# One more wait on SyncE: the seventh load of x is issued at a signal from TensorE's projection of the fifth group

## The chip, the cores and the metric

The kernel runs on one core of one Trainium2 chip. The metric is the device time of one execution in microseconds (us). A core has five engines with instruction streams of their own, which meet only at semaphores: TensorE (PE in the profile; its weight loads are PEld), VectorE (DVE), ScalarE (ACT), GpSimd (POOL) and SyncE (SP). Here SyncE does nothing but wait and issue DMAs. Every DMA of the kernel is issued there, on one queue, and the core's 16 DMA engines carry it out. SBUF is the on-chip memory, PSUM the one that TensorE writes, and HBM holds inputs and output.

## The reference

```python
def reference(x, A, B, scale):          # x: 16 x 512 x 768, A: 768 x 16, B: 16 x 768, scale 0.5
    lora = np.matmul(np.matmul(x, A), B)
    return (x + scale * lora).astype(np.float32)
```

The 16 x 512 rows are 8192 tokens of 768 numbers. x is read once (25.2 MB) and the output, as large, is written once. A and B are small.

## The kernel before

**Tiles and groups.** 128 tokens are a tile, so there are 64. They lie in SBUF in five parts of 8, 8, 16, 16 and 16 tiles (`PARTS`, L14). The SBUF buffer `x_sb` has room for the first four parts only (48 tiles, L61). The fifth part takes the places of the first two (L104): the first half of part 4 lands where part 0 was, the second half where part 1 was. The sums are written in place, so a place is free again when its part has been stored.

The computation goes by groups of 8 tiles, eight groups in all. For each group:

- ScalarE and GpSimd cast four tiles each from `x_sb` to 16-bit `xn` (L194). Before the first cast that touches a load they wait for that load's landing (L191), and for `s_taken` (L193): TensorE has begun to project the group before.
- VectorE transposes `xn` into `xt` (L250), 32 x 32 blocks at a time.
- TensorE projects: 24 matmuls (`MMS`, L127) with the weights from A, into the PSUM tile `ps_yt` (L281). Matmul m = 0 takes back a signal, m = 1 signals `s_taken`, the last (m = 23) signals `s_y`.
- ScalarE scales that and spreads it into `y_bd` (L238), four instructions.
- TensorE raises it by B in four pairs of tiles, four matmuls a pair, into two PSUM buffers `lora_ps` in turn (L302). The first matmul of pair 0 signals `s_raise`.
- VectorE adds each pair to `x_sb` (L255), four instructions a group.

On TensorE the groups overlap (L324 to L331): pairs 0 and 1 of group g, the first 12 matmuls of group g + 1's projection, pairs 2 and 3 of group g, then the other 12 matmuls. Group 0's projection stands alone ahead of the loop.

**The DMA order** is written out by hand in `on_sync` (L135 to L182). There are eight loads of x (`LOADS`, L106, numbered 0 to 7) and five stores (`STORES`, L128, 0 to 4), one for each part. Load 0 has two tiles and load 1 six; loads 2, 3, 4, 6 and 7 have eight tiles (3072 KB); load 5 has sixteen (6144 KB). Stores 0 and 1 have eight tiles, stores 2 to 4 sixteen. SP takes the steps strictly one after the other:

1. loads 0 and 1, then A and B, then loads 2 to 5;
2. signals that free PSUM buffers, and waits for the sums of parts 0 and 1;
3. a wait for TensorE's second pair of the third group (`s_lora`, L169), then stores 0 and 1;
4. a wait for store 0's landing (`s_out0`, L172), then load 6, which is the seventh and fills part 0's place;
5. a wait for store 1's landing (`s_out1`), then load 7;
6. for each of stores 2, 3 and 4 a wait for the part's last sum (L141), a signal to TensorE that a PSUM buffer is free (L144), and the store. Store 2 also waits until TensorE has begun to raise the sixth group (`s_raise`, L181).

A DMA adds 16 to its semaphore when it has landed as a whole.

Of the kernel before, what the change touches and what calls it, by code (L numbers as in the profile page):

```python
# [28 lines left out]
def kernel(  # L29
# [53 lines left out]
    def sem(name):  # L83
        sems.append(nc.alloc_semaphore(name))
        return sems[-1]
# [10 lines left out]
    def memory(t2, i, s, n):  # L96
        S = PARTS[i]
        return t2[ds(parts[i], S * P), :].rearrange("(p s) d -> p s d", s=S)[:, ds(s, n), :]

    def held(i, s, n):  # L100
        return tiles(where.index((i, s)), n)
# [19 lines left out]

    s_free = [sem(f"s_free{p}") for p in range(PAIRS)]
    s_out0, s_out1, s_raise = sem("s_out0"), sem("s_out1"), sem("s_raise")

    s_sum, s_out = sem("s_sum"), sem("s_out")

    MMS = 2 * NC  # L127
# [7 lines left out]
    def on_sync(e):  # L135
        def load(k):
            ld = LOADS[k]
            e.dma_start(out=held(*ld), in_=memory(x2, *ld)).then_inc(s_load[k], 16)  # L138

        def summed(k):  # L140
            e.wait_ge(s_sum, k + 1)  # L141
            if STORED[k] + 1 < NG:

                e.sem_inc(s_free[PAIRS - 1], 1)  # L144

        def store(k, done):
            st = STORES[k]
            e.dma_start(out=memory(out2, *st), in_=held(*st)).then_inc(done, 16)

        load(0)  # L150
        load(1)
        e.wait_ge(s_ready, 1)
        blocks = A.rearrange("(c e) r -> c (e r)", e=64)
        for c in range(SETS):
            e.dma_start(
                out=a_rows[c : SET * SET : SET, :], in_=blocks[ds(c * SET, SET), :]
            ).then_inc(s_a, 16)
        e.wait_ge(s_brows, 1)
        e.dma_start(out=b_rows[0 : R * APART : APART, :], in_=B).then_inc(s_b, 16)
        for k in range(2, len(LOADS) - 2):  # L160
            load(k)

        for p in range(2, PAIRS):
            e.sem_inc(s_free[p], 1)
        summed(0)
        summed(1)


        e.wait_ge(s_lora, 2 * PAIRS + 2)  # L169
        store(0, s_out0)  # L170
        store(1, s_out1)
        e.wait_ge(s_out0, 16)  # L172
        load(len(LOADS) - 2)
        e.wait_ge(s_out1, 16)
        load(len(LOADS) - 1)
        for k in range(2, len(STORES)):
            summed(k)
            if k == 2:


                e.wait_ge(s_raise, 6)  # L181
            store(k, s_out)  # L182
# [90 lines left out]
    def on_tensor(e):  # L273


        xv = xt.rearrange("p s (c j k) -> p s c j k", c=NC, k=2)

        def projected(first, last):
            for m in range(first, last):
                c, k = divmod(m, 2)  # L280
                mm = e.matmul(  # L281
                    y_ps, w_bd[:, c, k, :], xv[:, :, c, :, k],
                    start=(m == 0), stop=(m == MMS - 1),
                )
                if m == 0:
                    mm.then_inc(s_turned, -1)
                if m == 1:

                    mm.then_inc(s_taken, 1)
                if m == MMS - 1:  # L290
                    mm.then_inc(s_y, 1)

        def raised(p):
            if p == 0:
                e.wait_ge(s_spread, 1)
            free = s_free[(p + 2) % PAIRS]
            e.wait_ge(free, 1)
            t = lora[p % 2]
            mms = []
            for k in range(2):  # L300
                for n0, w in ((0, 512), (512, 256)) if k == 0 else ((0, 256), (256, 512)):
                    mms.append(e.matmul(  # L302
                        t[:, k, ds(n0, w)], y_bd[:, 2 * p + k, :], b_mm[:, ds(n0, w)],
                        start=True, stop=True,
                    ))
            if p == 0:
                mms[0].then_inc(s_raise, 1)
                mms[2].then_inc(s_spread, -1)
            mms[1].then_inc(free, -1)
            mms[-1].then_inc(s_lora, 1)  # L310

        e.wait_ge(s_pick, 2)
        e.wait_ge(s_bh, 1)
        for n0, w in ((0, 512), (512, 256)):
            last = e.matmul(  # L315
                lora[0][:, 0, ds(n0, w)], pick.rearrange("p b r -> p (b r)"),
                b_half[:, ds(n0, w)], start=True, stop=True,
            )
        last.then_inc(s_bp, 1)
        e.wait_ge(s_w, 1 + NQ)  # L320
        e.wait_ge(s_turned, 1)
        projected(0, MMS)
        e.wait_ge(s_bm, 1)
        with e.Fori(0, NG - 1):  # L324
            raised(0)
            raised(1)
            e.wait_ge(s_turned, 1)
            projected(0, MMS // 2)
            raised(2)
            raised(3)  # L330
            projected(MMS // 2, MMS)  # L331
        for p in range(PAIRS):
            raised(p)

    on_sync(nc.sync)
    on_gpsimd(nc.gpsimd)
    on_scalar(nc.scalar)
# [46 lines left out]
```

## Time and profile before

| what | value |
|---|---|
| median of 3 runs | 123.56 us (123.53 to 123.73) |
| the profiled execution | 123.76 us |
| its span, first to last instruction | 121.9 us |
| DMA engines busy, of 16 engines' span | 96.8%, 50.43 MB |
| VectorE busy | 81.7 us (67%) |
| TensorE busy (matmuls) | 50.5 us (41%) |
| ScalarE busy | 37.4 us (31%) |
| GpSimd busy | 28.4 us (23%) |
| SP waiting for a store's landing ahead of a load (L138) | 17.6 us in two waits, the longer 10.5 |

The profile comes from one execution, and its times count from the span's start. A group of instructions is written as line, engine, operation, output<-input. SPq is SP's sequencer: its DMA_DIRECT2D rows are the issues, not the transfers. A DMA is divided into packets on the 16 engines: a packet of a load or store of eight tiles has 24 KB, of sixteen tiles 48 KB, and each engine closes its share of a DMA with a packet under 512 B. The view of the DMA engines can be cut to a stretch of time and then says how many packets of each size began in it. "To landing" runs from the issue to the moment that the last engine's share is reported.

### The profile page before, as it was taken

How to read it: one execution, taken by the hardware profiler on the slowest of the kernel's cores; microseconds unless marked ns; L12 is line 12 of the kernel's file. 1: busy time of each engine (PE TensorE's matmuls, PEld its weight loads, DVE VectorE, ACT ScalarE, POOL GpSimd, SP SyncE). 2: the span in 40 equal slices, each digit the busy share in tenths (PEclk: the TensorE clock that was granted, in tenths of full speed). 3: DMA queues.
4: the chain of work that ended last, by engine and by line, in shares of the span. 5: the costliest groups of instructions: out<-in, count | busy, mean ns of one | idle time of the engine just before them, and what ended most of it. 6: DMA issues, size and time to landing. Idle time of an engine off the chain costs nothing.

```text
span 121.9 us, 885 instructions
## 1 busy us (share of the span) xinstructions
PE 50.5 (41%) x322; PEld 29.3 (24%) x322; DVE 81.7 (67%) x42; ACT 37.4 (31%) x43; POOL 28.4 (23%) x24
## 2 busy tenths in 40 slices
PE   0000239487457457647756714774674320000000
PEld 0000026244233233424424402442442110000000
DVE  0003850799999999999999959999995991000000
ACT  4003929444426402917230093643004000000000
POOL 7732638044026002607100090630000000000000
PEclk9999999999999999999999999999999985555555
DMA  3999999999997996999989999998998999899890
GB/s 67 421 429 429 443 443 403 451 435 419 476 516 339 435 516 298 460 403 443 443 363 460 427 427 468 451 484 387 419 500 387 403 516 403 371 516 419 355 516 0
DMA packets 1928, 50.43 MB, mean 414 GB/s; under 512 B 236, under 2 KB 236, under 8 KB 392
## 3 DMA queue, kind: packets, MB, share of 16 engines
q1 hardware_dynamic: 1928, 50.43, 96.8%
HBM read 25.26 MB, written 25.17 MB: 414 GB/s over the span
## 4 chain that ended last, share of the span: by engine, by line
DVE 33%; DMA 29%; PE 9%; ACT 6%; POOL 2%; issue 2%; SPq 0%; DVEq 0%
DVE x_sb L255 21%; DMA x_sb<-in_x_dram 20%; DVE xt L250 12%; DMA out_dram<-x_sb 9%; PE ps_yt L281 6%; ACT xn L194 3%; PE lora_ps L302 3%; ACT y_bd L238 2%; POOL xn L194 2%; SPq L138 0%; SPq L379 0%; DVEq L268 0%; SPq L133 0%
## 5 line engine op out<-in xcount | busy, mean ns | idle before, releaser
L255 DVE TENSOR_TENSOR x_sb<-x_sb,lora_ps 128x1536 f32<-128x1536 f32 x32 | 53.7, 1735 | 1.4 <-PE lora_ps L302 1.4
L302 PE MATMUL lora_ps<-b_mm,y_bd 128*128 128x512 f16 (+1 forms) x128 | 25.1, 328 | 23.7 <-ACT y_bd L238 15.3
L194 ACT CAST xn<-x_sb 128x3072 f16<-128x3072 f32 (+1 forms) x9 | 23.4, 2609 | 37.2 <-DMA x_sb<-in_x_dram 28.0
L250 DVE STREAM_TRANSPOSE xt<-xn 128x3072 f32<-128x3072 f32 (+1 forms) x9 | 27.0, 3005 | 6.7 <-PE ps_yt L281 4.9
L194 POOL CAST xn<-x_sb 128x3072 f16<-128x3072 f32 (+1 forms) x8 | 20.7, 2588 | 45.3 <-DMA x_sb<-in_x_dram 28.6
L281 PE MATMUL ps_yt<-xt,w_bd 128*128 128x256 f16 x192 | 25.7, 285 | 11.9 <-DVE xt L250 11.9
L281 PEld LDWEIGHTS ps_yt<-xt,w_bd 128*128 128x128 f16 x192 | 18.7, 100 | 19.6 <-issue 15.0
L302 PEld LDWEIGHTS lora_ps<-b_mm,y_bd 128*128 128x128 f16 x128 | 10.5, 97 | 36.8 <-ACT y_bd L238 17.5
L238 ACT ACTIVATE y_bd<-ps_yt 32x256 f16<-32x256 f32 x32 | 12.0, 374 | 17.7 <-PE ps_yt L281 17.4
L243 DVE STREAM_TRANSPOSE a_t<-a_rows 32x1024 f32<-32x1024 f32 x1 | 1.9, 1945 | 11.2 <-DMA a_rows<-in_A_dram 11.2
L315 PE MATMUL lora_ps<-b_half,pick 128*128 128x512 f16 (+1 forms) x2 | 0.8, 500 | 12.5 <-POOL b_half L212 12.5
L315 PEld LDWEIGHTS lora_ps<-b_half,pick 128*128 128x128 f16 x2 | 0.1, 105 | 12.5 <-issue 12.5
L220 POOL COPY w_bd<-w_one 32x384 f16<-32x384 f16 x4 | 2.0, 501 | 0.2
L212 POOL CAST b_half<-b_rows 128x768 f16<-128x768 f32 x1 | 0.8, 830 | 4.5 <-DMA b_rows<-in_B_dram 4.5
L194 ACT ACT_TABLE_LOAD x1 | 1.3, 1283 | 0.9 <-SPq L133 0.9
L202 POOL MEMSET w_bd<- 128x1536 f32 x1 | 1.4, 1372 | 0.0
L199 POOL MEMSET a_rows<- 32x1024 f32 x1 | 0.9, 941 | 0.5 <-SPq L133 0.5
L214 POOL CAST w_one<-a_t 32x384 f16<-32x384 f32 x1 | 0.8, 847 | 0.9 <-DVE a_t L243 0.9
L231 ACT CAST b_mm<-lora_ps 128x768 f16<-128x768 f32 x1 | 0.8, 798 | 0.0
L200 POOL MEMSET b_rows<- 128x768 f32 x1 | 0.7, 727 | 0.0
L203 POOL MEMSET y_bd<- 128x512 f32 x1 | 0.5, 514 | 0.0
L205 POOL TENSOR_SCALAR_AFFINE_SELECT pick<-pick 128x128 f16<-128x128 f16 x1 | 0.3, 300 | 0.0
(5 smaller groups left out, 0.6 us busy)
## 6 DMA issues: line engine op xcount, KB each, us to landing
out_dram<-x_sb SPq DMA_DIRECT2D x3, 6144.0 KB, 20.0
x_sb<-in_x_dram SPq DMA_DIRECT2D x5, 3072.0 KB, 14.8
x_sb<-in_x_dram SPq DMA_DIRECT2D x1, 6144.0 KB, 41.9
out_dram<-x_sb SPq DMA_DIRECT2D x2, 3072.0 KB, 14.9
x_sb<-in_x_dram SPq DMA_DIRECT2D x1, 2304.0 KB, 9.7
x_sb<-in_x_dram SPq DMA_DIRECT2D x1, 768.0 KB, 4.5
a_rows<-in_A_dram SPq DMA_DIRECT2D x3, 16.0 KB
b_rows<-in_B_dram SPq DMA_DIRECT2D x1, 48.0 KB, 7.4
```

The lines of the kernel that those rows point to most:

```text
L194: ins = copy(out=xn[:, ds(first, n), :], in_=tiles(t, n))
L199: e.memset(a_rows[0:Q], 0.0).then_inc(s_ready, 1)
L202: e.memset(w_bd.rearrange("p c k m -> p (c k m)").bitcast(fp32), 0.0)
L212: e.tensor_copy(out=b_half, in_=b_rows).then_inc(s_bh, 1)
L220: e.tensor_copy(out=w_bd[ds(b * Q, Q), :, :, ds(b * Q, R)], in_=w_one).then_inc(s_w, 1)
L238: last = e.mul(out=y_bd[q, :, q], in_=y_ps[q, :, :], mul=sc)
L243: e.transpose(out=a_t[0:Q].rearrange("i k r c -> i (k r) c"), in_=a_rows[0:Q].rearrange("c (i k r) -> c (k r) i", k=2, r=R),).then_inc(s_r ...
L250: return e.transpose(out=ts[0], in_=ts[1])
L255: ins = e.tensor_tensor(out=xs, in0=xs, in1=lora[p % 2], op=mybir.AluOpType.add)
L281: mm = e.matmul(y_ps, w_bd[:, c, k, :], xv[:, :, c, :, k], start=(m == 0), stop=(m == MMS - 1),)
L302: mms.append(e.matmul(t[:, k, ds(n0, w)], y_bd[:, 2 * p + k, :], b_mm[:, ds(n0, w)], start=True, stop=True,))
L315: last = e.matmul(lora[0][:, 0, ds(n0, w)], pick.rearrange("p b r -> p (b r)"), b_half[:, ds(n0, w)], start=True, stop=True,)
```

## The change

A semaphore `s_part` is added. TensorE's matmul with m = 20 (`MMS - 4`) adds one to it in each group's projection, so five is reached in the fifth group. SP waits for five between the wait for store 0's landing and the issue of load 6. Nothing else is changed: the order of the DMAs, their sizes and the work of the other engines are the same.

```diff
@@ -121,6 +121,7 @@
     s_out0, s_out1, s_raise = sem("s_out0"), sem("s_out1"), sem("s_raise")
+    s_part = sem("s_part")
@@ -170,6 +171,9 @@
         store(0, s_out0)
         store(1, s_out1)
         e.wait_ge(s_out0, 16)
+
+
+        e.wait_ge(s_part, 5)
         load(len(LOADS) - 2)
         e.wait_ge(s_out1, 16)
         load(len(LOADS) - 1)
@@ -287,6 +291,8 @@
                 if m == 1:
                     mm.then_inc(s_taken, 1)
+                if m == MMS - 4:
+                    mm.then_inc(s_part, 1)
                 if m == MMS - 1:
                     mm.then_inc(s_y, 1)
```

## The prediction

> **What bounds the kernel now.** I read the page's parts 1 to 3 first, then the chain in order of time, the timeline of the DMA queue's own engine, and last the DMA view cut into slices of 0.2 us.
>
> ```profile
> span 121.9 us, 885 instructions
> ...
> DMA  3999999999997996999989999998998999899890
> ...
> q1 hardware_dynamic: 1928, 50.43, 96.8%
> HBM read 25.26 MB, written 25.17 MB: 414 GB/s over the span
> ```
>
> The 16 DMA engines are busy 96.8% of the span, and what is missing lies mostly in the first and the last slice. VectorE, the busiest compute engine, has 67%. So the end is set by when the DMA engines run out of work, and a change counts only if one of them goes idle where it did not before, or the other way round. The chain names the transfers around the change:
>
> ```profile
> 43.92 11.36 DMA out_dram<-x_sb
> 55.28 0.02 issue
> 55.30 14.76 DMA x_sb<-in_x_dram
> 70.06 0.05 issue
> 70.11 2.76 POOL xn L194
> ```
>
> The first is store 0, landed at 55.28; the second is load 6 (the seventh), issued at 55.30 and landed at 70.06. Load 6 did not take 14.76 us because it is slow. It stood behind store 1, for the SP timeline has store 1 issued right after store 0, and load 7 released at 62.70 by store 1's landing:
>
> ```profile
> 43.92 0.82 SPq L148 DMA_DIRECT2D out_dram<-x_sb  x2
> 55.30 7.74 SPq L138 DMA_DIRECT2D x_sb<-in_x_dram  x2
> 74.87 26.51 SPq L148 DMA_DIRECT2D out_dram<-x_sb  x3
> ```
>
> The casts waiting on load 5 and load 7 start at 48.02 and 77.40. The landings 48.02, 55.28, 62.70, 70.06 and 77.40 lie 7.26, 7.42, 7.36 and 7.34 us apart, one transfer of 3072 KB each. So transfers run one behind the other in order of issue. What load 6 needs is only that its work is at each DMA engine when that engine has finished store 1, not that it was issued at 55.30.
>
> **The new wait: when it opens.** The fifth group is the projection whose second half stands here:
>
> ```profile
> 59.13 1.50 PE L281 MATMUL ps_yt<-xt,w_bd 128*128 128x256 f16 x12
> ```
>
> (The five second halves before the sixth group end at 21.9, 30.9, 40.8, 50.7 and 60.6; this is the last of them.) The matmul with m = 20 is the ninth of these twelve. Listed singly, matmuls start 0.11 us apart and this one at 60.02. The last of the twelve starts at 60.36 and ends at 60.63, so one lasts 0.27; the ninth ends at 60.29, and ScalarE follows the twelfth's signal 0.04 later (60.67). SP is thus released at about **60.33**, 5.03 us after 55.30.
>
> **Who waits behind it.** Behind the new wait on SP stand load 7, which waits for store 1's landing (62.70) anyway; then the signal that frees a PSUM buffer after group 3 (TensorE resumes on it at 63.15, 0.46 us idle); then stores 2 to 4, at 74.87, 83.08 and 101.04. All are bound to events later than 60.33: cost 0, with 2.4 us of cover at load 7. The added signal on matmul 20 costs nothing: the matmul with m = 1 carries a signal today and the starts stay 0.11 apart. No deadlock: projecting the fifth group needs data of load 4 and sums of earlier groups, not load 6. One more semaphore in a cleared range is no instruction more.
>
> **The step that matters: is load 6 there in time?** Each transfer ends with a small packet on each of the 16 DMA engines (under 512 B). In slices of 0.2 us these completions of store 1 count 3, 5, 4, 3, 1 from 61.40 to 62.40. This is the first slice that has any, 61.40 to 61.60:
>
> ```profile
> DMA packets 5, 0.05 MB, mean 246 GB/s; under 512 B 3, under 2 KB 3, under 8 KB 3
> ```
>
> Packets are counted where they start: at the end of the run the last 48 KB packets count at 118.6, 1.8 us ahead of the last completions at 120.4 to 120.6. So the first three DMA engines come free at 61.40 to 61.60, that is 1.07 to 1.27 us after the new issue; the others later, the last 1.9 or more.
>
> How long is issue to first packet? Two rows show it.
> (a) Store 2 is issued at 74.87, only just ahead of need. Its first packets, 48 KB, are in the slice 76.00 to 76.20:
>
> ```profile
> DMA packets 10, 0.25 MB, mean 1229 GB/s; under 512 B 4, under 2 KB 4, under 8 KB 4
> ```
>
> Ten packets: four completions of load 7, and six data packets averaging 41 KB, so four of 48 and two of 24. Four engines changed over without a gap, 1.13 to 1.33 us after the issue. And store 2 and load 7 lost nothing as a whole: 77.40 to 91.87 is 14.47 us for 6144 KB, 7.24 per 3072 KB.
> (b) Load 0 starts on idle engines, issued at 0.97: no packet until 1.80, 15 begun by 2.40, so 0.83 to 1.43 us. These first packets last 0.59 us on average (shares 0.25, 0.80, 1.72 of 16 engines in three slices of 0.2 us, over 15 packets) against 0.24 later (0.91 over 12), an extra 0.35.
>
> By (a), with almost the same lead, the loss is 0. By (b) there are three readings. As a whole: load 0 landed 4.5 us after issue, of which 768 KB at 7.34 us per 3072 KB are 1.83, so 2.67 is start and finish; load 6 alone on idle engines would land at 60.33 + 2.67 + 7.34 = 70.34, **0.28 late**. Engine by engine at the worst: one free at 61.40 whose work comes at 60.33 + 1.43 = 61.76 and whose first packet has the full extra 0.35: **0.71 late**. Paired kindly (the last to be fed is the last to be free): 0. Below zero: store 1, with load 6 queued behind it, took 0.16 more than store 0 (7.42 against 7.26); if the queued load did that, up to **0.16 gained**. I take 0.05, since (a) is the nearest row (a transfer issued just ahead of need, in mid-run) and the DMA engines that finish last have the most lead, 1.9 us.
>
> A rule of the Trainium skill speaks against the change: "DMA: Bandwidth & Descriptors", section "Rules for kernel authors", says to issue a DMA early so that its fixed setup cost overlaps. The same page, "Anatomy of one DMA — SWDGE (gpsimd) path", fits a DMA as about 2.0 us and its bytes at 436 GB/s (fitted for the other issue path). As an estimate from that page load 6 would land at 60.33 + 2.0 + 7.2 = 69.55, no later than today; load 0's row has 2.67 where the page has 2.0, and the measured figure decides.
>
> **Does a delay reach the end, and what is late next?** Yes, nearly whole. Load 6's landing releases the casts (70.08), then TensorE's sixth raise (74.45), then store 2 (74.87), whose lead of 1.13 us has nothing to spare; so a late landing can open a second gap there, but only on the DMA engines that finish load 7 first. Stores 3 and 4 have cover: store 3's first completions are at 105.0, store 4 is issued at 101.04, 3.96 us ahead, 2.6 more than (a) needed.
>
> **Sum.** Waiting on SP 0, signal 0, gap 0.05: span 121.9 becomes about 121.95. The profiled execution took 123.76 (1.86 outside the span), so it would take 123.81; it stands 0.20 above the median 123.56, and from the median I forecast **123.6**.
>
> **Rivals.** About 0.2% (0.25 us) is what a measurement of this kernel can tell from no change.
> 1. *The gap opens* (slower). DMA engines that finish store 1 first find an empty queue. It decides from the point where issue to first packet exceeds 1.07 to 1.27 us; (b) has up to 1.43 and the slow first packet. Price 0.28 to 0.71: 123.85 to 124.3, say 124.05. Against it: (a). For it: load 6 reads HBM, as load 0 did, while store 2 reads SBUF and may start sooner. The skill's page, section "Two DMAs through the same engine are not ordered", has reads and writes of one DMA engine in separate queues; load 6's first reads would then run during store 1's last writes only if issued early, which would add to this rival and is shown by no row.
> 2. *The late issue evens the DMA engines out* (faster). At the end ten of 16 finish by 120.0 and six only at 120.2 to 120.6; from the slices the mean is 120.0, the last about 120.5. If the early ones pause at 61.5 and the late ones speed up meanwhile, up to 0.5 comes off, and the 0.16 of store 1 may help: 123.05 to 123.3, say 123.25. Against it: with store 2's equally late issue the spread is no smaller afterwards (store 2's completions run from 90.4 to 91.6, load 7's from 76.0 to 77.2).
> 3. *The count is reached a group later than I count* (the sixth group's second half starts at 69.05, release near 70.25). The DMA engines would stand idle about 9 us: near 132. The code signals once per group, so this is remote. A release before 55.3, so that nothing changes, is equally remote: the fourth group's signal is near 50.4.
>
> **Numbers.** Forecast (within 0.2%, 123.35 to 123.8) 0.53; rival 1 0.31; rival 2 0.15; rival 3 0.01. Hence faster 0.15, same 0.53, slower 0.32. The range reaches to 0.55 of loss, into rival 1, and below to 0.25 of gain, leaving out the far ends: 123.3 to 124.1.
>
> **What would show it.** Right: load 6 issued at 60.3, landing still near 70.06; load 7 at 62.7; store 2 near 74.9; in the slices 61.4 to 62.4 each completion with a data packet beside it. Rival 1: fewer data packets than completions there, landing at 70.3 or later, store 2 and the end late by the same. Rival 2: store 1 landing before 62.6 or the last completions closer together. Wrong altogether: an issue of load 6 away from 60.3, or a difference that begins elsewhere than between 60 and 70 us.

## The result, and the profile after

| | before | changed |
|---|---|---|
| median | 123.59 us (6 runs, 123.47 to 123.84) | 125.06 us (6 runs, 124.48 to 125.46) |
| ratio | | 1.011, 95% interval 1.0087 to 1.0134 |
| the profiled execution and its span | 123.76, 121.9 | 125.27, 123.5 |

The change costs 1.1%, some 1.4 us. (Every ratio leaves out runs more than 1.5% above the fastest run of their kernel; only experiment 9 has such runs, two of six.) That is the prediction's rival 1 (the gap opens), at about twice the top of its price.

The page of the changed kernel first, the lines that answer to those shown of before:

```profile
span 123.5 us, 886 instructions
...
DMA  3999999999999798999899999997997999999790
...
q1 hardware_dynamic: 1928, 50.43, 96.2%
HBM read 25.26 MB, written 25.17 MB: 408 GB/s over the span
```

The same packets and bytes, but the execution takes 1.51 us longer (125.27 less 123.76; the spans, printed to 0.1, differ by 1.6). Slice 20, counted from 0 (61.7 to 64.8), has no striking digit, and that misleads: busy time counts a packet for as long as it lasts, and here packets last longer. The bytes show it better. SyncE's issues and two lines of the chain of waits give the place:

```profile
44.54 0.82 SPq L149 DMA_DIRECT2D out_dram<-x_sb  x2
61.00 1.65 SPq L139 DMA_DIRECT2D x_sb<-in_x_dram  x2
76.58 27.08 SPq L149 DMA_DIRECT2D out_dram<-x_sb  x3
```

```profile
61.00 10.55 DMA x_sb<-in_x_dram
71.55 0.02 issue
71.58 2.75 ACT xn L198
```

Load 6 is issued at 61.00 (55.30 before) and lands at 71.55 (70.06 before). Store 2, which hangs on that landing, moves from 74.87 to 76.58, and the end from 121.9 to 123.5. So 1.49 of the 1.51 us are there when load 6 lands.

Now the DMA engines in stretches of 1 us; the last two columns are their busy share, by where packets start, and GB/s. Before, then changed:

```profile
61.00:62.00 1.00, 0.00 (x0) 0.00 (x0) 1.00 (x2) 0.96 (x4) 0.00 (x0) 1.00 0.75 320
62.00:63.00 1.00, 0.75 (x4) 0.31 (x4) 1.00 (x1) 0.20 (x1) 0.00 (x0) 1.00 0.97 393
63.00:64.00 1.00, 0.90 (x5) 0.31 (x4) 1.00 (x1) 0.00 (x0) 0.00 (x0) 1.00 0.91 393
```

```profile
61.00:62.00 1.00, 0.24 (x3) 0.00 (x0) 1.00 (x1) 0.71 (x2) 0.00 (x0) 1.00 0.24 49
62.00:63.00 1.00, 0.14 (x1) 0.11 (x2) 1.00 (x2) 0.79 (x3) 0.00 (x0) 1.00 1.50 344
63.00:64.00 1.00, 1.00 (x8) 0.59 (x6) 1.00 (x1) 0.00 (x0) 0.00 (x0) 1.00 0.69 295
```

Over these 3 us the changed kernel starts 688 KB (49 + 344 + 295 GB/s, 1 us each) where the kernel before starts 1106. The missing 418 KB are 1.0 us at 430 GB/s, the rate of the kernel before from 74 to 76 us.

The packet counts show the two parts of the loss. In the changed kernel, 61.20 to 61.80 and then 61.80 to 62.60:

```profile
DMA packets 14, 0.00 MB, mean 0 GB/s; under 512 B 14, under 2 KB 14, under 8 KB 14
DMA packets 17, 0.37 MB, mean 461 GB/s; under 512 B 2, under 2 KB 2, under 8 KB 2
```

First, 14 of the 16 DMA engines report store 1 done in a stretch in which no packet of load 6 starts: they **stand idle**, on the mean from about 61.6 to 62.2, 0.6 us. Second, the first packets are **long**. Fifteen data packets start in the second stretch, and its DMA share there is:

```profile
61.80:62.60 0.80, 0.00 (x0) 0.00 (x0) 0.80 (x2) 0.78 (x3) 0.00 (x0) 1.00 2.01 461
```

2.01 of 16 engines over 0.80 us are 25.7 us, or 1.7 us a packet, where a 24 KB packet takes 0.91 in the steady flow (before, 63 to 64: 0.91 of 16 engines over 16 packets). That is 0.8 more; with the idle 0.6, 1.4 us.

These 1.4 us are the mean over the DMA engines, counted from their completions of store 1. The landing goes by the latest engine instead. Next, 62.60 to 63.20, then 69.80 to 70.40 and 70.40 to 71.40:

```profile
DMA packets 1, 0.02 MB, mean 41 GB/s; under 512 B 0, under 2 KB 0, under 8 KB 0
...
DMA packets 26, 0.34 MB, mean 574 GB/s; under 512 B 12, under 2 KB 12, under 8 KB 12
DMA packets 20, 0.39 MB, mean 393 GB/s; under 512 B 4, under 2 KB 4, under 8 KB 4
```

One DMA engine starts on load 6 only here, at 62.96. I follow the engines packet by packet: each engine's next packet begins where its last ended, which is how I assign them. By this the late starter is the one that finishes load 6 last, at 71.23, behind the twelve that are done by 70.40. Its packets after the first take 0.91 again, so time lost at the start is not made good.

### The profile page after: what moved, and what is told of

Its sections match the earlier page's. It is cut to its first block, busy times and chain, and to the rows that moved or that the text cites. A ratio compares the mean times of both kernels' runs of the same rounds, so it can differ in the third digit from the quotient of the medians.

```text
span 123.5 us, 886 instructions
## 1 busy us (share of the span) xinstructions
PE 52.8 (43%) x322; PEld 30.9 (25%) x322; DVE 81.8 (66%) x42; ACT 37.5 (30%) x43; POOL 28.4 (23%) x24
## 4 chain that ended last, share of the span: by engine, by line
DVE 43%; DMA 16%; PE 13%; ACT 8%; issue 3%; SPq 0%
DVE x_sb L259 28%; DMA x_sb<-in_x_dram 16%; DVE xt L254 15%; PE ps_yt L285 8%; ACT xn L198 6%; PE lora_ps L308 5%; ACT y_bd L242 2%; SPq L139 0%; SPq L385 0%; SPq L134 0%; SPq L176 0%
## 5 line engine op out<-in xcount | busy, mean ns | idle before, releaser
L308 PE MATMUL lora_ps<-b_mm,y_bd 128*128 128x512 f16 (+1 forms) x128 | 26.0, 340 | 23.6 <-ACT y_bd L242 16.2
L285 PE MATMUL ps_yt<-xt,w_bd 128*128 128x256 f16 x192 | 27.4, 298 | 12.0 <-DVE xt L254 12.0
L285 PEld LDWEIGHTS ps_yt<-xt,w_bd 128*128 128x128 f16 x192 | 19.7, 105 | 20.3 <-issue 15.1
L308 PEld LDWEIGHTS lora_ps<-b_mm,y_bd 128*128 128x128 f16 x128 | 11.1, 101 | 36.8 <-ACT y_bd L242 18.6
```

Of the source, the lines that this page charges most:

```text
L285: mm = e.matmul(y_ps, w_bd[:, c, k, :], xv[:, :, c, :, k], start=(m == 0), stop=(m == MMS - 1),)
L308: mms.append(e.matmul(t[:, k, ds(n0, w)], y_bd[:, 2 * p + k, :], b_mm[:, ds(n0, w)], start=True, stop=True,))
```

## The experiments

Theory 1: load 6 reaches the DMA engines too late; they run empty, start slowly, and every byte behind it is late by that. Rivals: the wait or the signal cost by themselves; the lower TensorE clock (0.897 against 0.909); a second gap at store 2. Ratios stand to the kernel before, run on the same chip, in 5 rounds.

**1. The same wait, signalled 18 matmuls earlier.**

```diff
-                if m == MMS - 4:
+                if m == 2:
```

> The signal is given by matmul m = 2 of each projection, not m = 20; wait and semaphore stay. TensorE's first half of the fifth projection began at 55.87 in the profile of the changed kernel, so SP is released near 56.4, about 5 us ahead of the first completion of store 1 (61.2). Theory 1 (load 6 comes too late at the DMA engines): no gap, 123.6, ratio to before 1.000 within 0.002. Rival (the added wait and signal cost by themselves, on SP or TensorE, or the lower TensorE clock of that execution does): stays near 125.0, ratio 1.011.

Measured 123.51 us, ratio 0.9998 (0.9985 to 1.0012). The wait and the signal cost nothing. Nor does the clock: the profiled execution of this kernel has the lower one and the shorter span (this kernel, then the changed one), and both pages show the same row of granted clock by slices, dip included:

```profile
PEclk9999999999999999999999995589999999555555
...
core 0: 121.5 us, clock 0.898
```

```profile
PEclk9999999999999999999999995589999999555555
...
core 0: 123.5 us, clock 0.897
```

**2. The signal eight matmuls earlier.**

```diff
-                if m == MMS - 4:
+                if m == MMS // 2:
```

> The signal is given by matmul m = 12, the first of the second half, eight starts of 0.11 us earlier: release near 60.1 in the phase of the changed kernel's profile, a lead of about 1.1 us over the first completion of store 1. Theory 1 with issue to first packet of 0.8 to 1.6 us: about 0.9 of the 1.47 us come back, 124.1 (123.9 to 124.4), ratio 1.004. If the lead of 1.13 us that store 2 shows is enough for a load too, all comes back, 123.6. Rival (wait and signal by themselves, or the clock): 125.0.

Measured 124.63 us (123.61 to 125.05), ratio 1.0079 (1.0055 to 1.0104). A miss, and the most useful one. Load 6 was issued at 59.59, 1.4 us ahead of the first completions, more than the lead the prediction counted on, and most of the loss stayed. Fifteen of the 16 DMA engines now go over to load 6 almost without a gap, and one does not. These are the stretches 61.00 to 61.80 (16 completions, 15 data packets), 61.80 to 62.10 and 62.70 to 62.80:

```profile
DMA packets 31, 0.37 MB, mean 461 GB/s; under 512 B 16, under 2 KB 16, under 8 KB 16
DMA packets 0, 0.00 MB, mean 0 GB/s; under 512 B 0, under 2 KB 0, under 8 KB 0
...
DMA packets 1, 0.02 MB, mean 246 GB/s; under 512 B 0, under 2 KB 0, under 8 KB 0
```

The loss shows when load 6 ends, 68.60 to 69.60 and then 70.00 to 70.80:

```profile
DMA packets 33, 0.47 MB, mean 467 GB/s; under 512 B 14, under 2 KB 14, under 8 KB 14
DMA packets 16, 0.34 MB, mean 430 GB/s; under 512 B 2, under 2 KB 2, under 8 KB 2
```

Fourteen DMA engines finish when they did before (there all 16 were done by 69.8); two come later, at 70.16 and 70.53. The load lands, and the kernel ends, with those two. Followed packet by packet, the one that ends at 70.16 started a packet at 62.66 that took 2.05 us. The one that ends at 70.53 is the engine without a packet: it started on load 6 only at 62.72, 3.1 us after the issue, having stood idle for 0.9 to 1.2 us.

**3. A later signal:** the start of the fifth group's raise.

```diff
-        e.wait_ge(s_part, 5)
+        e.wait_ge(s_raise, 5)
```

> SP waits for the fifth raise to begin (s_raise at 5) instead of s_part: release near 63.3 in the phase of the changed kernel's profile (62.87 there, and one matmul), 2.3 us later than there. Theory 1: every microsecond of lateness counts once the DMA engines are empty: 125.06 + 2.3 = 127.4 (126.9 to 127.7), ratio 1.030. Rival (a fixed price of the wait, of the clock, or of a second gap at store 2): 125 to 125.5.

Measured 126.68 us (126.20 to 127.22), ratio 1.0264 (1.0236 to 1.0292), somewhat under the range. In the profile the issue was at 62.37, not 63.3, and the first packets, 63.20 to 63.80, again took 1.7 us each (2.69 of 16 engines over 0.60 us, 15 packets). So lateness counts, and no fixed price explains 3 us.

**4. A signal between,** the third pair of the fourth group, and **5.** one between that and experiment 2, the casts of the sixth group.

```diff
-        e.wait_ge(s_part, 5)
+        e.wait_ge(s_lora, 3 * PAIRS + 3)     # 4
+        e.wait_ge(s_narrow, 10)              # 5
```

> In place of s_part, SP waits until the third pair of the fourth group has been raised (s_lora at 15), near 57.7 to 58.3: some 3 us ahead of the first completion of store 1, between the 5.3 us that cost nothing and the 1.4 us that cost 1.1. Theory 1 (load 6 must reach the DMA engines early enough that its first reads of HBM run behind store 1's last packets, some 2 us): no loss, 123.6 (123.4 to 123.8). Rival (a load must be queued as long before as possible, any later issue costs): 124.0 to 124.4.

> In place of s_part, SP waits for the tenth cast signal (s_narrow at 10: the casts of the sixth group are done), near 58.5 to 59.0: a lead of 2.2 to 2.8 us over the first completion of store 1, between 1.4 (cost 1.1) and 3.4 (cost 0.1). Theory 1 with a needed lead near 2 us: 123.6 to 123.8. If the price falls evenly from 1.4 to 3.4 us of lead: 124.0 to 124.2.

Measured: 4, 123.59 us, ratio 1.0011 (1.0000 to 1.0021). 5, 123.81 us (123.62 to 124.64), ratio 1.0034 (1.0016 to 1.0051). There is no sharp threshold at 2 us. The price fades out: in experiment 5 eight runs lie at 123.6 to 124.0 and three at 124.4 to 124.6. Together, with the ratio over the runs of each, and the lead as the one profiled execution of each has it (the start of the first 0.2 us slice with a completion of store 1, less the issue of load 6):

| kernel | issue | first completion | lead | ratio |
|---|---|---|---|---|
| experiment 1 | 56.03 | 61.2 | 5.2 us | 0.9998 |
| experiment 4 | 57.66 | 61.0 | 3.3 us | 1.0011 |
| experiment 5 | 58.15 | 61.2 | 3.0 us | 1.0034 |
| experiment 2 | 59.59 | 61.0 | 1.4 us | 1.0079 |
| the change | 61.00 | 61.2 | 0.2 us | 1.011 |
| experiment 3 | 62.37 | 61.6 | -0.8 us | 1.0264 |

**6 and 7. A piece of load 6 ahead of the wait,** one tile or two, as it was issued before the change; the rest behind the wait.

```diff
-        (0, 0, 2), (0, 2, 6), (1, 0, 8), (2, 0, 8), (2, 8, 8), (3, 0, 16), (4, 0, 8), (4, 8, 8)
+        (0, 0, 2), (0, 2, 6), (1, 0, 8), (2, 0, 8), (2, 8, 8), (3, 0, 16), (4, 0, 1), (4, 1, 7), (4, 8, 8)
...
+        load(len(LOADS) - 3)
         e.wait_ge(s_part, 5)
```

(With two tiles (4, 0, 2), (4, 2, 6); the loop of the early loads ends one sooner.)

> Load 6 is cut in two: one tile (384 KB) is issued at store 0's landing as before the change, the other seven after the wait of the changed kernel. The tile gives each DMA engine 8 packets of 3 KB, about 0.9 us of work, behind store 1. Theory 1: the gap shrinks by that 0.9 us and the seven tiles have a lead of 1.1 to 1.3 us instead of 0.2 to 0.4: 123.8 (123.5 to 124.3), ratio 1.002. Rival (the late wait costs by something other than empty DMA engines): stays near 125.

> As the run with one tile ahead of the wait, but with two tiles (768 KB, 1.8 us of work) ahead and six behind. The six then have a lead of some 2.1 us, and the DMA engines are already reading HBM when they arrive. Theory 1 with a needed lead near 2 us: 123.6 to 123.8, against 124.1 with one tile. If the late second piece costs whatever its lead: stays near 124.1.

Measured: one tile 124.11 us, ratio 1.0051 (1.0034 to 1.0068); two tiles 123.93 us, 1.0030 (1.0012 to 1.0047). The wait is as late as in the change (the rest issued at 60.73 and 60.30), and half to three quarters of the loss are gone when the DMA engines have a piece of work in between. That is theory 1 from its other side; two tiles fell a little short of what was expected.

**8. A store issued late instead,** in the kernel before.

```diff
-                e.wait_ge(s_raise, 6)
+                e.wait_ge(s_lora, 5 * PAIRS + 2)
```

> The kernel before, but store 2 waits for the second pair of the sixth group (s_lora at 22) instead of the first matmul of that group's raise: issue near 76.0 instead of 74.87, lead over the first completion of load 7 about 0. Theory 1a (an idle gap of 0.8 to 1.0 us, and the slow first packets of load 6 belong to reads of HBM): 124.4 (124.1 to 124.7), first 48 KB packets of 1.8 to 1.9 us as in the kernel before. Rival 1b (whatever starts on empty DMA engines has slow first packets): 125.0 or more, first packets of 2.5 us.

Measured 124.65 us (123.60 to 124.97), ratio 1.0080 (1.0048 to 1.0112). Store 2 was issued at 76.56, after the first completions of load 7. The stretch 77.40 to 77.60:

```profile
DMA packets 15, 0.74 MB, mean 3686 GB/s; under 512 B 0, under 2 KB 0, under 8 KB 0
...
77.40:77.60 0.20, 0.20 (x3) 0.13 (x2) 0.20 (x1) 0.18 (x1) 0.15 (x1) 0.50 8.69 3686
```

Fifteen DMA engines start at once (the sixteenth just before, in 77.20 to 77.40), 0.84 to 1.04 us after the issue, and a 48 KB packet takes 1.85 us (8.69 of 16 engines over 0.20 us, 15 packets) against 1.81 for the first packets of store 2 in the kernel before. This is what theory 1a expected. A late store pays its idle gap only. A late load pays the gap, long first packets, and a few DMA engines that start much later than the rest.

**9. Load 7 issued late,** behind a load instead of a store, in the kernel before. The signal that frees a PSUM buffer after group 3 goes ahead of it, so that TensorE doesn't wait for it.

```diff
         e.wait_ge(s_out1, 16)
-        load(len(LOADS) - 1)
         for k in range(2, len(STORES)):
             summed(k)
             if k == 2:
+                e.wait_ge(s_lora, 4 * PAIRS + 3)
+                load(len(LOADS) - 1)
```

> The kernel before, but load 7 is issued late instead of load 6: SP first passes on the signal that frees the PSUM buffer after group 3, then waits for the third pair of the fifth group (s_lora at 19, near 67.6) and issues load 7, about 1.0 to 1.3 us ahead of the first completion of load 6 (68.6 to 68.8) instead of 6. It stands behind a load, so the DMA engines are reading HBM when it arrives. If a short lead costs a load whatever runs ahead of it: about 1.0 us, 124.5 (124.2 to 124.9), as with 1.4 us of lead behind a store. If the price lies in the change from a store to a load: 123.6 to 123.9.

Measured ratio 1.0155 (1.0117 to 1.0192), six runs from 124.67 to 127.11: more than either answer. So the price does not belong to the change from a store to a load. The profiled execution is one of the two that the ratio leaves out (127.10 us), so what follows holds for it alone: load 7 was issued at 67.79, 0.9 us ahead of load 6's first completion, most DMA engines took it up at 68.8 to 69.6, and two only at 70.45 and 71.03 by the packets, 2.7 and 3.2 us after the issue.

**10 and 11. Store 2 without its wait for the sixth raise,** in the changed kernel and in the one before.

```diff
-            if k == 2:
-                e.wait_ge(s_raise, 6)
```

> The changed kernel without store 2's wait for the sixth raise, so store 2 is issued soon after load 7 (near 62.8) instead of at 76.6. Theory 1 (all of the loss arises where load 6 starts): unchanged, 125.0 (124.6 to 125.4). Rival (the late load 6 makes store 2 late, and part of the loss arises there a second time): 124.3 or less.

> The kernel before without store 2's wait for the sixth raise: store 2 issued near 63 instead of 74.87. If a store needs no more than the 1.13 us that it has there: unchanged, 123.55 within 0.25. If a store loses time to so late an issue as a load does: faster, 122.5 to 123.2.

Measured: 10, 126.51 us (125.91 to 127.36), ratio 1.0239 (1.0207 to 1.0271); 11, 123.89 us (123.40 to 124.65), ratio 1.0032 (1.0016 to 1.0047). Both miss, on the other side: issuing store 2 early costs time itself. So experiment 10 cannot tell whether a late store 2 had a part in the loss; the profile of the change can, for there 1.49 of the 1.51 us are lost before store 2 is issued. In 10 load 7's last packets are what grows. The first line is the kernel before, the second experiment 10:

```profile
74.00:76.00 2.00, 1.47 (x8) 0.70 (x8) 2.00 (x1) 0.38 (x2) 0.00 (x0) 1.00 1.00 430
```

```profile
74.00:78.00 4.00, 2.23 (x8) 1.16 (x9) 3.71 (x2) 1.66 (x5) 0.18 (x1) 0.51 0.99 301
```

The DMA engines are as busy (1.00 and 0.99) and move 301 GB/s instead of 430.

## Why the prediction was wrong, step by step

- **What bounds the kernel** held: the DMA engines' work one behind the other, and what is late there is late at the end. So did the costs set at nothing: the wait and the signal (experiment 1), and what stands behind the wait on SP (in the change load 7 was still issued at store 1's landing, 62.32).
- **When the wait opens** came out 0.67 us late: 61.00, not 60.33. In the profiled execution the first projection took 5.28 us (4.76 before), and the second half of the fifth began 0.61 later (59.74, not 59.13); store 1's first completions came at 61.2, not 61.4. The lead of 1.07 to 1.27 us was the difference of two times of one execution that do not move together: TensorE's progress and the DMA engines'. In the change it was 0.2. The four profiled executions with this wait have the issue behind it at 60.30, 60.73, 60.92 and 61.00 (experiments 7, 6 and 10, and the change), so the forecast lay at the early end of a spread of 0.7. This accounts for the idle 0.6 us, but not for the whole outcome, for in experiment 2 the lead was 1.4 us and 0.8% were lost all the same.
- **The step that failed** is "By (a), with almost the same lead, the loss is 0", and "I take 0.05, since (a) is the nearest row". Row (a) is store 2. Experiment 8 shows what it could not: even a store that finds the DMA engines empty starts on 15 of them within 0.2 us with packets of normal length. Load 6 does not. The nearer row was (b), the only load that starts on empty engines. The text noted the difference (SBUF against HBM) under rival 1 and gave it too little weight.
- **The size in rival 1** was too small by half (0.28 to 0.71 against about 1.4). The term is the extra of a first packet: 0.35 us came from load 0's 6 KB packets and was used for 24 KB, where it measured 0.8 (1.7 against 0.91). (Row (b) itself is read almost rightly: by the packets, one of its 15, at 2.31, is an engine's second.) And the estimate of 0.71 took the worst DMA engine to start 1.43 us after the issue; by the packets, stragglers started 2.0 us (the change) and 3.1 us (experiment 2) after it.
- **"The DMA engines that finish last have the most lead"** was no protection. Experiment 2 shows it: two engines are delayed, each finishes its own share behind the other fourteen, and the late two make the landing late.
- **The rule weighed against the change** (the Trainium skill, "DMA: Bandwidth & Descriptors", section "Rules for kernel authors": issue a DMA early so that its fixed cost is covered) was right for load 6, whose price goes from 0 at a lead of 5.2 us to 1.1% at 0.2. Experiments 10 and 11 have the contrary: store 2 issued 12 us earlier made the kernel before slower by 0.3%. The same page's fit for the other issue path (2.0 us and the bytes at 436 GB/s) gives as an estimate a landing of load 6 9.2 us after its issue; it took 10.55.
- **What would show it** did: fewer data packets than completions from 61.2 on, the landing past 70.3, store 2 and the end late by about as much (1.7 and 1.5 us). The issue away from 60.3, listed there under "Wrong altogether", came as well, by 0.67.

Open: why a few DMA engines take up a load so late, and whether the long first packets come from reading HBM. Load 6 and store 2 differ in packet size as well as in direction, and no run separated the two. Why the early store 2 stretches the last packets of load 7 was not pursued either; the loss was largest where load 6 had been late as well.

## What to carry to other kernels

Where the DMA queue sets the end, a load must be queued well before the DMA engines come to it: here 3.3 us were enough and 1.4 were not, though a store did with 1.1. Earlier is not always better: the store issued 12 us earlier cost time (experiment 11). A lead that is the difference of a compute time and a DMA time should be taken with the spread of both over several executions, not from one profile. And a row that stands in for an unmeasured cost must match it in direction and packet size, or its result is a bound and not a value.

## What the runs showed of the hardware that was not expected

- A load that arrives at empty DMA engines: first 24 KB packets of 1.7 us instead of 0.91, in the change and in experiment 3. A store (experiment 8): 1.85 us instead of 1.81 for 48 KB.
- Even with a lead of 1.4 us, 2 of 16 DMA engines finished a load 0.6 and 1.0 us after the last of the others, and one of the two had started it 3.1 us after the issue (experiment 2).
- With a store queued behind a load from soon after the load's issue on, the load's last packets were slow: 301 GB/s at full busy share in experiment 10, and a ratio of 1.0239 against the 1.011 of the change, whose store 2 waits.
